# A transformer block on one core: operand sums in steps, keys as side work, elementwise work off GpSimd, recurrence and decays in turn, longer pauses

## The chip, the cores and the metric

The kernel runs on one core of one Trainium2 chip. The metric is device time in microseconds for one execution; the time before is 1280.81 us, the median of three runs (1280.46 to 1280.88). The engines are TensorE (PE, with its weight loads as PEld), VectorE (DVE), ScalarE (ACT), GpSimd (POOL) and SyncE (SP, which here only issues DMAs).

## What is computed

One block on 512 tokens of width 1024, in float32:

```python
x = layer_norm(ALPHA * x + 0.5 * swiglu(x, ffn1_w1, ffn1_w3, ffn1_w2), ln1_g, ln1_b)
x = layer_norm(ALPHA * x + token_mixer(x, w_in, b_in, ...), ln2_g, ln2_b)
x = layer_norm(ALPHA * x + 0.5 * swiglu(x, ffn2_w1, ffn2_w3, ffn2_w2), ln3_g, ln3_b)

# token_mixer
q_a, k_a, v_a, f_h, q_h, i_h, og_h, gate_a, gate_h = split(x @ w_in + b_in)
y_attn = sliding_window_attention(rope(q_a), rope(k_a), v_a, sinks)   # 16 heads of 64, 4 key heads, window 128
o_h = hgrn2_recurrence(silu(q_h), f_h, i_h, lb)                       # 8 heads of 128, chunks of 64
y_h = rms_norm(o_h) * norm_g * silu(og_h)
mix = (sigmoid(gate_a) * (y_attn @ w_pa) + sigmoid(gate_h) * (y_h @ w_ph)) @ w_out
```

The two feed-forward layers have 2816 hidden columns.

## The kernel before, in words

Activations are held with features on partitions and 512 tokens in the free dimension. Every float32 operand of a large product is split into a rounded high part and a remainder (`split`: a copy on ACT into `whi`, then a subtraction on DVE into `wlo`), and a product is three matmuls: high by high, high by low, low by high (`mm3`, or the inner loop of `Quads.mul`).

The wide projections use a seven-product scheme of the Winograd kind on 2x2 blocks (`Quads.quad`): for each pair of 256-column weight groups it loads four raw weight tiles, forms sums of them on DVE (`plus`, tile `wsum`), splits seven operands, and multiplies them in turn with seven forms of the input: the blocks b11, b21, b22 and the sums t1, t2, t3, t4 of blocks. The order of products is f1 (b11), f5 (t1), f6 (t2), f2 (b21), f7 (t3), and, together with the next call's first product, m4 (t4) and m3 (b22). `X` holds the input blocks and their sums; `X.mixed` forms t1 to t4 once for each of the three inputs (first feed-forward, mixer, second feed-forward), with the low parts of t3 and t4 subtracted on POOL. `eight` is the plain first pass of a feed-forward layer, during which `mixed` runs.

The mixer goes through these stages in the code: values and keys (`v_tile`, `k_half`); bias, rotation and split of the keys (`rope`, one multiplication of which is on POOL); `x1.mixed`; the projections of queries (`q_quad`), gates (`gate_quad`) and recurrence inputs (`quad_to`, `vals`); two output projections (`sums`); the last product with its normalization (`down_and_norm`).

Attention and the recurrence are "side work": Python generators in one queue (`Side`). After half and at the end of each product the planner's `tick` adds `rate` times a share to what is due and takes that many steps of the generator; a step that yields `PAUSE` ends that tick's steps, while what is due is kept. `attention` prepares two query tiles (`q_parts`) and interleaves one chunk of score, softmax and value work (`scores`, `probs`, `weigh`) with the next preparation (`both`). `heads` runs, for each head of the recurrence, `decays` (elementwise preparation on DVE and ACT) and then, one head later, `recur` (score products, transposes, updates, output products, a normalization whose inverse root is a `pow` on POOL, transposes, gate). A scheduler then sets, at build time, the order in which each engine's instructions finally stand, from the code's order and its own idea of durations; every engine runs its instructions in that order.

Lines to follow: L71 to L76 `split`; L125 to L149 `fin` and `mixed`; L284 the matmuls of `mul`; L299 `plus`; L304 `keep` (m1, vs, u3: copies of a product's bank by ACT before the bank is used again); L655 to L661 `rope`; L690 to L697 the keys; L721 the query's low part; L738 and L739 scores; L769 the probabilities' scaling; L992, L994 the recurrence's output products; L997 to L1007 its normalization and the transposes behind.

Of the kernel before, what the change touches and what calls it, by code (L numbers as in the profile page):

```python
# [15 lines left out]
ALU = mybir.AluOpType  # L16
# [26 lines left out]
def body(ctx, tc, a):  # L43
# [73 lines left out]
    class X:  # L117
# [8 lines left out]
        def fin(self, n, c, src, eng=None):  # L126
            t = self.op[n][:, :, :, c]
            nc.scalar.copy(out=t[:, 0], in_=src)
            (eng or nc.vector).tensor_tensor(out=t[:, 1], in0=src, in1=t[:, 0], op=ALU.subtract)  # L129

        def mixed(self, room):
            pool = nc.gpsimd
            full = slice(0, 256)
            b11, b12, b21, b22 = (self.plain[k] for k in ("b11", "b12", "b21", "b22"))

            def tmp():
                return room().rearrange("p (k c) -> p k c", k=4)
# [4 lines left out]
            self.fin("t1", full, t1)  # L142
            t4 = tmp()
            nc.vector.scalar_tensor_tensor(out=t4, in0=t2, scalar=-1.0, in1=b21, op0=ALU.mult, op1=ALU.subtract)
            self.fin("t2", full, t2)
            t3 = tmp()
            nc.vector.tensor_tensor(out=t3, in0=b22, in1=b12, op=ALU.subtract)
            self.fin("t3", full, t3, pool)
            self.fin("t4", full, t4, pool)  # L149
# [108 lines left out]
    class Outs:  # L258
# [3 lines left out]
        def room(self, i):  # L262
            return self.rooms[i]
# [4 lines left out]
    class Quads:  # L268
# [63 lines left out]
        def quad(self, src, outs):  # L332
# [3 lines left out]
            p1 = self.plus(w21, w22)  # L336
            p3 = self.plus(w11, w21)
            v, c, m1, vs, u3, p2, p4 = ([] for _ in range(7))
# [10 lines left out]
            def g2():  # L349
                p2.append(self.plus(w22, p3))  # L350
                return wsplit(p2[0])
# [26 lines left out]
            pipe.push(lambda: wsplit(p3), f7)  # L378
            self.late = (v, c, w22, p4, u3, vs, outs)

        def eight(self, src, finish, stages=()):
# [22 lines left out]
            self.x.mixed(self.sum_room)  # L404
# [221 lines left out]
    def quad_to(src, d1, d2, done=None):  # L626
# [5 lines left out]
        quads.quad(src, Outs((*thalves(d1), d2[:, :, 256:]), finish))  # L632
# [48 lines left out]

    top, bot = slice(0, HD), slice(HD, P)
# [546 lines left out]
```

## Time and profile before

| | before |
|---|---|
| median of the runs | 1280.81 us |
| profiled execution: own time | 1279.68 us |
| profiled execution: span, first to last instruction | 1277.8 us |
| PE busy | 1239.9 us, 97% |
| DVE busy | 934.7 us, 73% |
| ACT busy | 628.3 us, 49% |
| POOL busy | 74.1 us, 6% |
| mean granted TensorE clock | 0.995 of full speed |

The profiled execution's own time is 1.88 us above its span, and the median of the runs 1.13 us above that. Matmuls of this kernel overlap with the weight loads of the next ones, so PE counts as busy whenever one of them is under way, and its idle time is where it waits for an operand, a free bank, or nothing at all at the two ends. A row of the timeline gives start and duration in us, engine, line, operation and tiles, and in square brackets the idle time before it and what ended that.

### The profile page before, as it was taken

The page shows a single profiled execution, that of the slowest core. Times are in us where ns is not written, and L with a number is a line of the kernel's source. Part 1 is how long each engine was busy: PE and PEld are TensorE (multiplying, and loading weights), DVE is VectorE, ACT ScalarE, POOL GpSimd, SP SyncE. Part 2 cuts the span into 40 slices and gives each one's busy share as a digit, 9 for nine tenths or more (in the row PEclk, how much of TensorE's full clock was granted, in tenths as well). Part 3 has the DMA queues.
Part 4 walks back from the last instruction along what each step waited for, and adds up shares of the span by engine and source line. Part 5 has one row for each costly group of instructions (what it writes and reads, how often), then busy time and mean ns, then how long its engine had stood idle before and what let it go on. Part 6 is the DMA issues. An engine that isn't in the chain of part 4 may idle for free.

```text
span 1277.8 us, 21726 instructions
## 1 busy us (share of the span) xinstructions
PE 1239.9 (97%) x9040; PEld 1167.8 (91%) x9040; DVE 934.7 (73%) x1288; ACT 628.3 (49%) x891; POOL 74.1 (6%) x53
## 2 busy tenths in 40 slices
PE   8999999999998999999999999999999999999997
PEld 7999999988898999989999988788899999998886
DVE  7987878723399998998778786564898788784325
ACT  5645455511155677687653746442365445462110
POOL 2000000000031100100100010000110000000001
PEclk9999999999999999999999999999999999999998
DMA  6424233523233335223223243664333323343211
GB/s 242 138 95 132 84 116 116 183 97 99 90 112 100 114 118 157 83 87 123 72 78 105 83 148 124 223 206 132 116 101 114 116 92 108 118 162 132 95 38 66
DMA packets 51139, 150.75 MB, mean 118 GB/s; under 512 B 5728, under 2 KB 12896, under 8 KB 51040
## 3 DMA queue, kind: packets, MB, share of 16 engines
q1 hardware_dynamic: 47008, 135.72, 32.6%
q10 hardware_dynamic: 4032, 13.63, 3.0%
q8 instruction: 71, 1.16, 0.4%
q14 instruction: 28, 0.23, 0.1%
HBM read 134.65 MB, written 14.68 MB: 117 GB/s over the span
## 4 chain that ended last, share of the span: by engine, by line
PE 52%; DVE 11%; issue 2%; ACT 2%; POOL 1%; DVEq 0%; POOLq 0%; ACTq 0%
PE A L284 27%; PE A L106 4%; PE A L107 4%; PE A L108 4%; DVE wlo L75 2%; PE B L107 2%; PE B L106 2%; PE B L108 2%; PE B L113 2%; DVE wsum L299 2%; PE B L961 1%; PE B L790 1%; POOL rs L1003 1%; DVE g L721 1%; DVE r L743 1%
## 5 line engine op out<-in xcount | busy, mean ns | idle before, releaser
L284 PE MATMUL A<-x,whi 128*128 128x256 f32 x3840 | 551.2, 286 | 12.2 <-ACT whi L74 6.3
L284 PEld LDWEIGHTS A<-x,whi 128*128 128x128 f32 x3840 | 500.6, 193 | 15.7 <-ACT whi L74 6.6
L75 DVE TENSOR_TENSOR wlo<-raw,whi 128x1024 fp32r<-128x1024 f32 (+1 forms) x186 | 225.6, 1215 | 191.4 <-ACT whi L74 191.2
L74 ACT CAST whi<-raw 128x1024 fp32r<-128x1024 f32 (+1 forms) x186 | 192.7, 1040 | 313.7 <-PE A L108 115.0
L284 PE MATMUL A<-x,wlo 128*128 128x256 f32 x1920 | 312.4, 285 | 1.6 <-DVE wlo L75 1.6
L284 PEld LDWEIGHTS A<-x,wlo 128*128 128x128 f32 x1920 | 267.3, 193 | 2.0 <-DVE wlo L75 2.0
L74 ACT CAST whi<-wsum 128x1024 fp32r<-128x1024 f32 x128 | 134.5, 1051 | 146.3 <-PE A L284 91.5
L75 DVE TENSOR_TENSOR wlo<-wsum,whi 128x1024 fp32r<-128x1024 f32 x128 | 156.2, 1220 | 11.9 <-ACT whi L74 11.7
L106 PE MATMUL A<-whi,x 128*128 128x256 f32 (+1 forms) x360 | 115.7, 321 | 0.0
L107 PE MATMUL A<-wlo,x 128*128 128x256 f32 (+1 forms) x360 | 115.6, 321 | 0.0
L108 PE MATMUL A<-whi,x 128*128 128x256 f32 (+1 forms) x360 | 114.9, 320 | 0.0
L299 DVE TENSOR_TENSOR wsum<-raw 128x1024 f32<-128x1024 f32 x64 | 87.4, 1372 | 2.7 <-POOL x L129 2.0
L299 DVE TENSOR_TENSOR wsum<-raw,wsum 128x1024 f32<-128x1024 f32 x64 | 78.1, 1220 | 0.8
L106 PEld LDWEIGHTS A<-whi,x 128*128 128x128 f32 x360 | 68.5, 190 | 5.0
L108 PEld LDWEIGHTS A<-whi,x 128*128 128x128 f32 x360 | 68.3, 190 | 4.9
L107 PEld LDWEIGHTS A<-wlo,x 128*128 128x128 f32 x360 | 68.5, 190 | 4.5
L107 PE MATMUL B<-wlo,x 128*128 128x512 f32 (+1 forms) x200 | 69.8, 349 | 0.0
L106 PE MATMUL B<-whi,x 128*128 128x512 f32 (+1 forms) x200 | 69.7, 348 | 0.0
L108 PE MATMUL B<-whi,x 128*128 128x512 f32 (+1 forms) x200 | 69.4, 347 | 0.0
L420 POOL TENSOR_TENSOR rstd<-ve,pw 128x1 f32<-128x1 f32 x12 | 16.2, 1351 | 761.2 <-DVE ve L418 760.0
L106 PE MATMUL A<-x,whi 128*128 128x512 f32 (+1 forms) x160 | 59.5, 372 | 0.0
L108 PE MATMUL A<-x,wlo 128*128 128x512 f32 (+1 forms) x160 | 59.3, 371 | 0.0
(171 smaller groups left out, 1520.2 us busy)
## 6 DMA issues: line engine op xcount, KB each, us to landing
raw<-in_w_dram SPq DMA_DIRECT2D x130, 512.0 KB, 3.6
raw<-in_w_fqg_dram SPq DMA_DIRECT2D x24, 512.0 KB, 3.5
raw<-in_w_q_dram SPq DMA_DIRECT2D x8, 512.0 KB, 3.6
raw<-in_w_ga_dram SPq DMA_DIRECT2D x8, 512.0 KB, 3.9
raw<-in_w_gh_dram SPq DMA_DIRECT2D x8, 512.0 KB, 3.7
raw<-in_w_i_dram SPq DMA_DIRECT2D x8, 512.0 KB, 3.9
raw<-in_w_pa_dram SPq DMA_DIRECT2D x8, 512.0 KB, 4.8
g<-x_spill ACTq DMA_DIRECT2D x8, 512.0 KB, 4.8
```

Of the source, the lines that this page charges most:

```text
L74: nc.scalar.copy(out=hi, in_=src)
L75: nc.vector.tensor_tensor(out=lo, in0=src, in1=hi, op=ALU.subtract)
L106: nc.tensor.matmul(out, lhsT=lh, rhs=rh, start=first, stop=False, **kw)
L107: nc.tensor.matmul(out, lhsT=lh, rhs=rl, start=False, stop=False, **kw)
L108: nc.tensor.matmul(out, lhsT=ll, rhs=rh, start=False, stop=last, **kw)
L113: nc.tensor.transpose(out=tp[:, j * P:(j + 1) * P], in_=b, identity=ident)
L284: nc.tensor.matmul(reg, lhsT=w, rhs=x, start=first, stop=last, skip_group_check=True)
L299: nc.vector.tensor_tensor(out=t, in0=x, in1=y, op=ALU.add)
L420: nc.gpsimd.tensor_tensor(out=rstd, in0=ve, in1=pw, op=ALU.pow)
L721: nc.vector.tensor_tensor(out=q[other, h], in0=t[own], in1=q[own, h], op=ALU.subtract)
L743: nc.vector.tensor_tensor_reduce(out=neg[hf][:, i, :kb * P], in0=sc[hf][:, i * 256:i * 256 + kb * P], in1=amask[:, koff:], scale=-(HD ** - ...
L790: mm = nc.tensor.matmul(o[hf][hf * HD:(hf + 1) * HD, i * 256:(i + 1) * 256], lhsT=v_sb[:, n + i + 1 - kb + kk, g * HD:(g + 1) * HD], rhs=p ...
```

## The change

- `X.mixed` becomes a generator of four steps with three given rooms instead of four rooms from a ring; all low parts are subtracted on DVE, and t3 is written over t1. In the feed-forward layers it runs in one go at the place where it ran before; in the mixer its four steps stand between the pushes of the first `quad` (the queries).
- The keys get only their bias at the entry; rotation and split become a generator `k_parts`, side work at rate 1 beside the first gate projection, ahead of `attention` in the queue. The zeroing of the unused key halves moves with it.
- `rope` multiplies by the sine on DVE, not on POOL. After the change POOL keeps the `pow` of the normalizations, the copies of the recurrence and the memsets.
- `probs` pauses twice before its transposes instead of once; `attention` pauses twice before each chunk; `both` takes a preparation step at every third step of the chunk instead of every fourth.
- `recur` pauses after the squares' sum (a plain yield before) and twice, not once, before its last transposes.
- `heads` deals out `recur` of one head and `decays` of the next step by step; before, all of `decays` came first, and then `recur`. The rates of the first three pairs of heads go from 4 to 5.

```diff
-        def mixed(self, room):
-            pool = nc.gpsimd
+        def mixed(self, rooms):
...
-            t1, t2 = tmp(), tmp()
+            t1, t2, t4 = (t.rearrange("p (k c) -> p k c", k=4) for t in rooms)
             nc.vector.tensor_tensor(out=t1, in0=b11, in1=b12, op=ALU.subtract)
+            self.fin("t1", full, t1)
+            yield
...
-            self.fin("t3", full, t3, pool)
-            self.fin("t4", full, t4, pool)
+            self.fin("t4", full, t4)
+            yield
...
+            if not mix:
+                s1()
+                s3()
             pipe.push(lambda: wsplit(w11), f1)
+            if mix:
+                next(mix)
+                s1()
             self.flush()
-            pipe.push(lambda: wsplit(p1), f5)
+            pipe.push(lambda: wsplit(p1[0]), f5)
+            if mix:
+                next(mix)
+                s3()
             pipe.push(g2, f6)
             pipe.push(g4, f2)
+            if mix:
+                next(mix)
+            pipe.push(lambda: wsplit(p3[0]), f7)
+            if mix:
+                next(mix)
...
-    def rope(src, b, sign, dst):
-        nc.scalar.activation(out=dst, in_=src, func=AF.Identity, bias=b, scale=sign)
+    def rope(dst):
         rot = room(0)
         nc.vector.stream_shuffle(out=rot, in_=dst, mask=swap)
-        nc.gpsimd.tensor_tensor(out=rot, in0=rot, in1=sin_t, op=ALU.mult)
+        nc.vector.tensor_tensor(out=rot, in0=rot, in1=sin_t, op=ALU.mult)
...
-    x1.mixed(quads.sum_room)
+    mix = x1.mixed([big(i, [P, 1024]) for i in (2, 4, 10)])
+    k_hi, k_lo = [], []
+
+    def k_parts():
...
+        for j in range(2):
+            t = k_raw[j]
+            rope(t)
+            yield
...
-        yield PAUSE
+        for _ in range(2):
+            yield PAUSE
         tps = [transposed([neg[j // 2][:, j % 2, kk * P:(kk + 1) * P] for j in range(4)]) for kk in range(kb)]
...
         for i in range(4):
+            for _ in range(2):
+                yield PAUSE
             if i < 3:
-                nxt = yield from both(chunk(i // 2, i % 2, qs), q_parts((i + 1) // 2, (i + 1) % 2), 4)
+                nxt = yield from both(chunk(i // 2, i % 2, qs), q_parts((i + 1) // 2, (i + 1) % 2), 3)
...
-    q_quad(0)
+    q_quad(0, mix)
+    side.add(k_parts())
+    side.rate = 1.0
     gate_quad(0)
     pipe.pump()
     side.add(attention())
...
         nc.vector.tensor_reduce(out=ss, in_=sq.rearrange("p (t e) -> p t e", e=P), axis=AX.X, op=ALU.add)
-        yield
+        yield PAUSE
...
-        yield PAUSE
+        for _ in range(2):
+            yield PAUSE
         oT = transposed([on[:, t * P:(t + 1) * P] for t in range(TT)])
...
         for h in (2 * pr, 2 * pr + 1):
-            d = yield from decays(h)
+            if ahead:
+                h0, d = ahead.pop()
+                d = yield from both(recur(h0, *d), decays(h), 1)
+            else:
+                d = yield from decays(h)
             ahead.append((h, d))
-            if len(ahead) > 1:
-                h0, d = ahead.pop(0)
-                yield from recur(h0, *d)
-                yield
+            yield
```

What this does to the order of the instructions is shown at three places, all on DVE, which PE waits for there.

The mixer's entry before, from t3's sum (L147) to the first key's split (L696); `wlo<-raw` is the first weight tile's low part, the r tiles are the keys.

```order
L147 TENSOR_TENSOR wsum<-g_3475,g_3473 128x1024
L299 TENSOR_TENSOR wsum<-raw 128x1024
L621 TENSOR_TENSOR g_3696<-A,bv_c 128x256
L299 TENSOR_TENSOR wsum<-raw 128x1024
L75 TENSOR_TENSOR wlo<-raw,whi 128x1024
L658 STREAM_SHUFFLE r_3933<-r_3931 128x512
L75 TENSOR_TENSOR wlo<-wsum,whi 128x1024
L660 TENSOR_TENSOR r_3931<-r_3931,rope_c_c 128x512
L299 TENSOR_TENSOR wsum<-raw,wsum 128x1024
L661 TENSOR_TENSOR r_3931<-r_3931,r_3933 128x512
L299 TENSOR_TENSOR wsum<-raw,wsum 128x1024
L696 TENSOR_TENSOR g_3925<-r_3931,g_3923 64x512
```

The same stretch now, from t1's low part (x_3477); x_3478 and x_3480 are the low parts of t2 and t3, L138 and L142 their sums.

```order
L75 TENSOR_TENSOR x_3477<-g_3926,x_3477 128x1024
L297 TENSOR_TENSOR wsum<-raw 128x1024
L138 SCALAR_TENSOR_TENSOR g_3927<-g_3926,g_3474 128x1024
L297 TENSOR_TENSOR wsum<-raw 128x1024
L142 TENSOR_TENSOR g_3926<-g_3474,g_3472 128x1024
L75 TENSOR_TENSOR wlo<-raw,whi 128x1024
L637 TENSOR_TENSOR g_3695<-A,bv_c 128x256
L75 TENSOR_TENSOR x_3478<-g_3927,x_3478 128x1024
L75 TENSOR_TENSOR wlo<-wsum,whi 128x1024
L297 TENSOR_TENSOR wsum<-raw,wsum 128x1024
L75 TENSOR_TENSOR x_3480<-g_3926,x_3480 128x1024
L297 TENSOR_TENSOR wsum<-raw,wsum 128x1024
```

The keys' rotation and split have left this stretch, the operand sums stand among the weight sums, and the sum for the third product (`wsum<-raw,wsum`) comes with no key work ahead of it. The first product's low part stands ahead of t2's low part.

The queries of the second half of attention before: shuffle (L658), cosine product (L660), sum (L661), low parts (L721); the sine product between L658 and L661 is on POOL.

```order
L658 STREAM_SHUFFLE r_5613<-g_5130 128x512
L299 TENSOR_TENSOR wsum<-raw 128x1024
L660 TENSOR_TENSOR g_5130<-g_5130,rope_c_c 128x512
L75 TENSOR_TENSOR wlo<-raw,whi 128x1024
L661 TENSOR_TENSOR g_5130<-g_5130,r_5613 128x512
L658 STREAM_SHUFFLE r_5655<-g_5130 128x512
L75 TENSOR_TENSOR wlo<-raw,whi 128x1024
L721 TENSOR_TENSOR g_5618<-g_5130,g_5618 64x512 x2
```

And now, with the sine product as L674.

```order
L673 STREAM_SHUFFLE r_5611<-g_5047 128x512
L297 TENSOR_TENSOR wsum<-raw 128x1024
L674 TENSOR_TENSOR r_5611<-r_5611,rope_s_c 128x512
L675 TENSOR_TENSOR g_5047<-g_5047,rope_c_c 128x512
L75 TENSOR_TENSOR wlo<-raw,whi 128x1024
L676 TENSOR_TENSOR g_5047<-g_5047,r_5611 128x512
L75 TENSOR_TENSOR wlo<-raw,whi 128x1024
L746 TENSOR_TENSOR g_5616<-g_5047,g_5616 64x512 x2
```

One DVE instruction is added for each rotation; the rest keeps its order.

The second of the eight recurrence heads before, from the scaling by the inverse root (L1005), for which PE's transposes wait; L930 to L945 are decays of the head after the next one, L964 the start of the next one's recurrence.

```order
L1005 TENSOR_TENSOR r_7515<-B,rs 128x512
L930 TENSOR_TENSOR g_7543<-r_7540 128x8x64
L937 TENSOR_TENSOR dd<-r_7542 128x4
L938 TENSOR_TENSOR g_6819<-g_6819,r_7542 128x512
L1011 SCALAR_TENSOR_TENSOR r_7535<-B,norm_g_c,g_6414 128x512
L939 TENSOR_TENSOR g_7543<-g_7543,r_7539 128x8x64
L940 TENSOR_TENSOR g_7543<-g_7543,r_7539 128x8x64
L945 TENSOR_TENSOR r_7582<-g_6819,r_7542 128x4x64
L621 TENSOR_TENSOR g_7461<-A,bv_c 128x256
L964 COPY_PREDICATED g_6407<-amask_c,B 128x512
```

The same place now, from L1035, which is that scaling; L956, L960 and L967 are decays of the head after the next one, L994 and L998 the start of the next one's recurrence.

```order
L1035 TENSOR_TENSOR r_7499<-B,rs 128x512
L956 SCALAR_TENSOR_TENSOR r_7547<-rope_c_c,r_7548 128x512
L297 TENSOR_TENSOR wsum<-raw 128x1024
L960 TENSOR_TENSOR g_7550<-r_7547 128x8x64
L297 TENSOR_TENSOR wsum<-raw 128x1024
L1042 SCALAR_TENSOR_TENSOR r_7533<-B,norm_g_c,g_6412 128x512
L994 COPY_PREDICATED g_6405<-amask_c,B 128x512
L998 TENSOR_TENSOR g_7363<-g_7363,r_7362 128x3x64
L967 TENSOR_TENSOR dd<-r_7549 128x4
L637 TENSOR_TENSOR g_7471<-A,bv_c 128x256
```

Those decays are at an earlier point here: their scan (L956) and the work behind it stand after the scaling, and the next head's recurrence starts among them. On PE the number of large matmuls between a head's last output product and its transposes goes, head by head, from 35, 37, 21, 33, 23, 15, 20, 13 to 27, 44, 36, 41, 36, 20, 24, 18 (256 columns each for the first five heads, 512 for the last three).

## Rows read from the trace of the kernel before

**Rows 1.** The page's busy times: us, share of the span, instructions.

```profile
PE 1239.9 (97%) x9040; PEld 1167.8 (91%) x9040; DVE 934.7 (73%) x1288; ACT 628.3 (49%) x891; POOL 74.1 (6%) x53
```

**Rows 2.** PE's waits by line and releaser: us in total, times, longest.

```profile
PE B L113 <- DVE r L1005: 7.7, 8, 1.5
PE A L284 <- ACT whi L74: 6.3, 2, 5.6
PE A L284 <- ACT m L304: 5.6, 3, 3.7
PE B L738 <- DVE g L721: 3.0, 3, 2.2
PE B L113 <- DVE r L769: 2.6, 4, 1.4
PE A L284 <- DVE wlo L75: 1.6, 2, 0.9
```

**Rows 3.** Timeline of PE: stops in both feed-forward layers and the mixer's entry.

```profile
39.08 1.21 PE L284 MATMUL A<-x,whi 128*128 128x256 f32 x8 [1.24 <-ACT m L304]
...
396.27 1.32 PE L284 MATMUL A<-x,whi 128*128 128x256 f32 x8 [3.66 <-ACT m L304]
...
944.52 0.74 PE L284 MATMUL A<-x,wlo 128*128 128x256 f32 x4 [0.64 <-DVE wlo L75]
```

**Rows 4.** Stretches: length, busy us (count) by engine, granted clock, DMA share, GB/s.

```profile
396.00:400.00 4.00, 3.73 (x21) 3.73 (x22) 3.94 (x5) 3.16 (x4) 1.35 (x1) 0.65 0.00 0
400.00:404.00 4.00, 4.00 (x33) 4.00 (x32) 4.00 (x5) 3.69 (x6) 0.00 (x0) 0.92 0.43 131
532.00:536.00 4.00, 3.94 (x23) 3.75 (x24) 3.91 (x7) 1.24 (x2) 0.00 (x0) 0.72 0.47 165
536.00:540.00 4.00, 4.00 (x31) 4.00 (x31) 3.85 (x14) 2.41 (x8) 1.30 (x1) 0.85 0.02 7
```

**Rows 5.** Stretches of attention, output projection and second feed-forward layer.

```profile
420.00:480.00 60.00, 57.50 (x471) 54.57 (x470) 59.15 (x139) 42.55 (x97) 7.13 (x4) 1.00 0.36 118
820.00:830.00 10.00, 10.00 (x45) 8.26 (x44) 6.54 (x6) 6.85 (x8) 0.00 (x0) 1.00 1.00 382
1000.00:1100.00 100.00, 100.00 (x836) 100.00 (x835) 80.09 (x80) 49.58 (x61) 0.00 (x0) 1.00 0.33 106
```

**Rows 6.** Timeline of the mixer's entry: POOL's low parts and DVE's weight sum.

```profile
378.48 6.82 POOL L129 TENSOR_TENSOR x<-wsum,x 128x1024 fp32r<-128x1024 f32 x2 [10.34 <-ACT x L128]
...
382.97 3.40 DVE L299 TENSOR_TENSOR wsum<-raw 128x1024 f32<-128x1024 f32 x1 [1.97 <-POOL x L129]
```

**Rows 7.** Timeline of the second feed-forward layer: the same two.

```profile
936.49 5.76 POOL L129 TENSOR_TENSOR x<-wsum,x 128x1024 fp32r<-128x1024 f32 x2 [10.28 <-ACT x L128]
...
937.14 6.20 DVE L299 TENSOR_TENSOR wsum<-raw 128x1024 f32<-128x1024 f32 x2
```

**Rows 8.** DVE in attention by line: busy us, mean ns, idle before.

```profile
L75 DVE TENSOR_TENSOR wlo<-wsum,whi 128x1024 fp32r<-128x1024 f32 x24 | 29.2, 1216 | 0.4 <-ACT whi L74 0.3
...
L660 DVE TENSOR_TENSOR g<-g,rope_c_c 128x512 f32<-128x512 f32 x8 | 7.2, 903 | 0.0
L661 DVE TENSOR_TENSOR g<-g,r 128x512 f32<-128x512 f32 x8 | 5.5, 682 | 0.0
```

**Rows 9.** Timeline of attention's second half: the longest score wait.

```profile
530.36 2.36 DVE L721 TENSOR_TENSOR g<-g,g 64x512 fp32r<-64x512 f32 x2
...
532.06 0.33 PE L738 MATMUL B<-g,g 128*128 128x128 f32 x1 [2.16 <-DVE g L721]
```

**Rows 10.** Timeline of a head's normalization, from its last output products.

```profile
674.76 0.38 PE L994 MATMUL B<-r,r 128*128 128x128 f32 x2
...
678.59 1.02 POOL L1003 TENSOR_TENSOR rs<-ss,pw 128x4 f32<-128x4 f32 x1 [11.21 <-DVE ss L1001]
...
679.64 0.69 DVE L1005 TENSOR_TENSOR r<-B,rs 128x512 f32<-128x512 f32 x1 [0.81 <-POOL rs L1003]
...
680.39 0.66 PE L113 MATMUL B<-ident,r 128*128 128x128 f32 x4 [0.82 <-DVE r L1005]
```

More of the change, by code (lines that the diff above doesn't have):

```diff
@@ L330, in done, with quad, s1, s3 @@
             pipe.pump()
-        def quad(self, src, outs):
+        def quad(self, src, outs, mix=None):
             w11, w21, w22, w12 = (raw(src[i]) for i in (0, 2, 3, 1))
-            p1 = self.plus(w21, w22)
-            p3 = self.plus(w11, w21)
-            v, c, m1, vs, u3, p2, p4 = ([] for _ in range(7))
+            v, c, m1, vs, u3, p1, p2, p3, p4 = ([] for _ in range(9))
+            def s1():
+                p1.append(self.plus(w21, w22))
+            def s3():
+                p3.append(self.plus(w11, w21))
             def f1(w):
@@ L349, in g2 @@
             def g2():
-                p2.append(self.plus(w22, p3))
+                p2.append(self.plus(w22, p3[0]))
                 return wsplit(p2[0])
@@ L403, in eight @@
             self.mul(c1[1], w[1], "b22", False, True)
-            self.x.mixed(self.sum_room)
+            for _ in self.x.mixed([self.sum_room() for _ in range(3)]):
+                pass
             c2[1] = bank("A")
@@ L684, in body, with q_quad @@
     top, bot = slice(0, HD), slice(HD, P)
-    k_hi = [big(i, dtype=F32R) for i in (4, 10)]
-    k_lo = [big(i, dtype=F32R) for i in (2, 11)]
-    for t in k_lo:
-        nc.gpsimd.memset(t[top, 1].bitcast(F32), 0.0)
-        nc.gpsimd.memset(t[bot, 0].bitcast(F32), 0.0)
-    for j in range(2):
-        t = room(6 + j)
-        rope(accs[j], bias("k", j), 1.0, t)
-        for h, own in enumerate((top, bot)):
-            for half in (top, bot):
-                nc.scalar.copy(out=k_hi[j][half, h], in_=t[own])
-            nc.vector.tensor_tensor(out=k_lo[j][own, h], in0=t[own], in1=k_hi[j][own, h], op=ALU.subtract)
-    x1.mixed(quads.sum_room)
+    k_raw = [room(6 + j) for j in range(2)]
+    for j in range(2):
+        nc.scalar.activation(out=k_raw[j], in_=accs[j], func=AF.Identity, bias=bias("k", j), scale=1.0)
+    mix = x1.mixed([big(i, [P, 1024]) for i in (2, 4, 10)])
+    k_hi, k_lo = [], []
+    def k_parts():
+        k_hi.extend(big(i, dtype=F32R) for i in (4, 10))
+        k_lo.extend(big(i, dtype=F32R) for i in (2, 11))
+        for t in k_lo:
+            nc.gpsimd.memset(t[top, 1].bitcast(F32), 0.0)
+            nc.gpsimd.memset(t[bot, 0].bitcast(F32), 0.0)
+        for j in range(2):
+            t = k_raw[j]
+            rope(t)
+            yield
+            for h, own in enumerate((top, bot)):
+                for half in (top, bot):
+                    nc.scalar.copy(out=k_hi[j][half, h], in_=t[own])
+                nc.vector.tensor_tensor(out=k_lo[j][own, h], in0=t[own], in1=k_hi[j][own, h], op=ALU.subtract)
+                yield
     q_raw = {}
-    def q_quad(pp):
+    def q_quad(pp, mix=None):
         d = [big(i) for i in range(2)]
@@ L705, in done @@
             q_raw[pp] = d
[L706 removed]
+        quad_to(a["w_q"][pp], d[0], d[1], done, mix)
     def q_parts(pp, ip):
@@ L715, in q_parts @@
             t = q_raw[pp][ip][:, i]
-            rope(t, bias("q", 4 * pp + 2 * ip + i), 1.0 if ip == 0 else -1.0, t)
+            nc.scalar.activation(out=t, in_=t, func=AF.Identity, bias=bias("q", 4 * pp + 2 * ip + i),
+                                 scale=1.0 if ip == 0 else -1.0)
+            rope(t)
             yield
@@ L1040, in body @@
     vals(0)
-    next_heads(0, 4.0)
+    next_heads(0, 5.0)
     quad_to(a["w_fqg"][2], pairs[1].q, pairs[1].g)
@@ L1044, in body @@
     pairs[2] = Pair(0)
-    next_heads(1, 4.0)
+    next_heads(1, 5.0)
     quad_to(a["w_fqg"][3], pairs[2].f, pairs[2].q)
@@ L1051, in body @@
     quad_to(a["w_fqg"][4], pairs[2].g, pairs[3].f)
-    next_heads(2, 4.0)
+    next_heads(2, 5.0)
     quad_to(a["w_fqg"][5], pairs[3].q, pairs[3].g)
```

23 lines of the change are left out of this document (9 added, 14 removed).

## The prediction, made before the changed kernel was run

> **What bounds the kernel now.** I read the page's busy times first, then PE's waits, then PE's timeline around each of them, then the stretches for the clock, and last DVE's and POOL's rows at the waits. PE is busy 1239.9 of 1277.8 us [rows 1]: a stop of PE lengthens the run by itself, and what the other engines do counts only where PE waits for it. The span holds 37.9 us without PE. Of this 6.3 us are waits for `whi` [rows 2] at the very start, which the change leaves alone. What it can reach is in the five other lines: 7.7 us before the recurrence's transposes, 5.6 for copies of a bank (m1), 3.0 before scores, 2.6 before attention's transposes, 1.6 for a `wlo` [rows 2]; 20.5 us together. The remaining 11 us are the end of the run and small gaps. The longest are one of 3.66 us at the mixer's entry [rows 3] and one of 2.16 us before scores [rows 9].
>
> Behind these two long stops PE's granted clock is at 0.65, 0.92 and at 0.72, 0.85 in four stretches of 4 us [rows 4], that is, partly at 1.2 instead of 2.4 GHz; everywhere else around it is 1.00. Lost work: 4 x (0.35 + 0.08) = 1.7 us and 4 x (0.28 + 0.15) = 1.7 us. So at most 20.5 + 3.4 = 23.9 us are to be had, which is 1257 us.
>
> In a steady stretch 836 matmuls take 100 us, 0.12 us each [rows 5]; in the output projections, with 512 columns, 45 take 10 us, 0.22 each. These two paces turn counts of matmuls in the new order into time.
>
> **Operand sums.** The change takes two subtractions of 128x1024 per input from POOL and puts them on DVE: 2 x 1.22 = 2.4 us more for DVE [rows 8]. POOL needs 5.8 to 6.8 us for the two [rows 6, 7], and DVE suffers meanwhile: two weight sums that are worth 2.4 us take 6.2 [rows 7], 3.8 lost; at the entry one takes 3.4 instead of 1.2 after 1.97 us of waiting for POOL's result [rows 6], 4.2 lost. So DVE gets back 3.8 to 4.2 for 2.4 and is 1.3 us or more earlier at the next `wlo`. PE's stops behind these places are 1.24 us in the first feed-forward layer, 0.64 [rows 3] and 0.7 (the third of the three waits for m1: 5.6 - 1.24 - 3.66) in the second. The 1.24 and 0.7 are waits for ACT's copy m1, which stands behind a cast of a weight sum that DVE had late; in the new order m1 stands ahead of that cast in the second layer. I take all 2.6 us as gained; bounds 0 and 2.6.
>
> The Trainium skill speaks against the direction of this: "Perfetto Trace Analysis", section "Optimizing Scalar/DVE Operations", says that work of a saturated DVE may be offloaded, even to GpSimd, and adds that the two share a port, so that it might not help. By the first half the moved work would cost DVE 2.4 us per input and 5.5 us for the queries with nothing back, which is the slower case below; rows 7, with 6.2 us for 2.4 us of work, side with the second half.
>
> **The mixer's entry.** Before, the key rotation and split stand among the first product's operands, and DVE reaches the sum for the third product only behind them; PE stops 0.95 us (1.6 - 0.64) for the first `wlo` and 3.66 us for m1. In the new order t1's low part, the weight sums and the first five weight splits come without key work. The first `wlo` is five DVE operations of at most 1.22 us behind t1's low part, without POOL's 4.2 us; the operand of each later product is ready one product (24 matmuls, 2.9 us) or more ahead. I take both stops as gone, 4.6 us, and the clock behind the second, 1.7; bounds 2 and 6.3. Key rotation and split then run beside the first gate product; nothing but attention's first score waits for them, and that comes 24 matmuls later in PE's order than before.
>
> **Attention.** The eight sine products leave POOL: 8 x 0.68 = 5.5 us more on DVE [rows 8], which is full there, 59.15 of 60 us [rows 5]. Back come the cosine products' excess, 8 x (0.903 - 0.682) = 1.8 us [rows 8], and 1.0 us for each pair of low parts that meets a rotation (2.36 instead of 1.36 us [rows 9]). So DVE has 1 to 4 us more in some 180 us, and this is the term with the worst cover. But each rotation becomes shorter by what POOL took over 0.68, and the 2.16 us [rows 9] are just such a chain: its low parts alone end 1.0 us late. Of the score and transpose waits (3.0 + 2.6) I take 3.6 as gained: attention's 16 groups of transposes still stand right behind the last scaling on DVE, and I charge an eighth of a microsecond for each (an estimate from 2.6 us for 16 such groups before, four of which waited). The second clock stretch goes with the 2.16: 1.5 of 1.7. Bounds for the whole: -6 (all that DVE is given, in front of PE) and 7.3. Two more pauses per block and per chunk delay attention; in the new PE order its end is 37 matmuls nearer to the first recurrence head, with main matmuls still between its last steps (21, 14, 12), so nothing is left over that PE would have to wait through.
>
> **The recurrence.** Between a head's last output product and its transposes stand the square, its sum, the `pow`, the scaling, and other DVE work. One head: output products end at 675.14, transposes start at 680.39, so 5.25 us, against 37 matmuls x 0.12 = 4.4 us, and 0.82 us of waiting [rows 10]. DVE itself loses 0.81 us there to the `pow`. The counts change by -8, +7, +15, +8, +13 (x 0.12) and +5, +4, +5 (x 0.22). Setting each new count against its chain, with the new neighbours on DVE, leaves about 0.7, 0, 0, 0.6, 0.1, 1.3, 0, 0 = 2.7 us. What DVE loses to a `pow` does not vanish where PE no longer waits: behind the second head its queue is dense (a scan, two weight sums, then the next head's first steps), and I expect the 0.8 us again before the next transposes. So 7.7 - 2.7 - 0.8 = 4.2 us gained; bounds -1 and 7.7.
>
> **Sum.** 2.6 + 6.3 + 3.6 + 1.5 + 4.2 = 18.2 us. The profiled execution's own time, 1279.68 us, would become 1261.5; it is 1.13 us below the median of the runs, so the median of 1280.81 becomes about 1263 us.
>
> **Rivals.**
> - Nearly everything goes: DVE, no longer held up by POOL, is ahead of PE all through the mixer. For it speaks that seven of the eight heads' counts grow, by 0.8 to 1.8 us, against a mean wait of 7.7 / 8 = 1.0; against it that DVE goes on losing 0.8 us to a `pow` [rows 10]. 1257 us.
> - The waits move: operand sums and entry gain their 8.9 us, but in attention and recurrence each stop that a pause removes comes back at the next score, update or transpose, since DVE is as late as before. For it speaks DVE's 59.15 of 60 us, against it that rows 2 name no wait for an update or an output product. 1272 us.
> - The pauses don't bite: the scheduler fills with the same matmuls as before where the chain is on DVE, as for the sixth head, and the recurrence gains nothing. 1267 us.
> - Slower: DVE becomes the bound from the entry to the end of attention. It is given 2.4 (operands) + 10 x 0.68 (rotations) = 9.2 us in that stretch; if next to nothing comes back from POOL, PE waits that long for `wlo`, the entry's gain is lost with it, and only the recurrence's 4.2 us stand against it: 1286 us. It decides where less than half of the excess in rows 6 to 9 is owed to POOL. By the rule named above it would be the likely one; here rows 6 and 7 show the excess only while POOL runs.
>
> **Chances.** Forecast (1260 to 1266) 0.45; nearly everything 0.15; pauses don't bite 0.13; waits move 0.2; slower 0.05; the rest within a few microseconds of before. The range that leaves out about 2 in 10: 1257 to 1271. A measurement of this kernel tells 0.2% (2.6 us) from no change: faster 0.92, within 0.03, slower 0.05.
>
> **What would show it.** In the new profile: no stop over 0.3 us at the entry and a clock of 1.00 there; no PE wait behind the operand sums; DVE's weight sums at 1.22 us all through; rotations without stretched neighbours; PE's waits for the scaled rows at about 3 us in eight, and for attention's scaling at about 2. Wrong would be: new waits for `wlo` in attention, a wait of PE for the updates (L1016) or for keys, DVE rows as long as before with POOL idle, or PE idle in the mixer as long as before.

## The result, and the profile after

| | before | after |
|---|---|---|
| time, median | 1280.85 us (1280.46 to 1281.72, 4 runs) | 1266.68 us (1265.33 to 1268.93, 4 runs) |
| ratio to before, 95% interval | | 0.9891 [0.9877, 0.9905] |
| profiled execution, own time and span | 1279.68, 1277.8 | 1268.93, 1267.1 |

The changed kernel is 14.2 us (1.1%) faster; 17.8 were forecast (1263), and 1266.68 lies inside the range 1257 to 1271. (The median of before has one run more here than ahead of the prediction.) The profiled execution is the longest of the four. Its own time is 10.75 us below that of before, so what follows is set against 10.75; the spread between runs is taken up in the last section.

The page's busy times of the kernel after answer to [rows 1]: us, share of the span, instructions.

```profile
PE 1239.7 (98%) x9040; PEld 1168.6 (92%) x9040; DVE 929.1 (73%) x1304; ACT 628.5 (50%) x891; POOL 37.5 (3%) x37
```

PE's work is the same; the span without PE goes from 37.9 to 1267.1 - 1239.7 = 27.4 us, 10.5 us less, nearly all of the 10.75. DVE has 16 instructions more and yet 5.6 us less to do.

PE's waits of the kernel after, by line and releaser (us in total, times, longest), against [rows 2]. L282, L113, L763 and L1035 are L284, L113, L738 and L1005 of before; `whi` at the top is again mostly the start of the run (5.79 and 1.15 us; 5.55 and 0.75 before).

```profile
PE A L282 <- ACT whi L74: 7.2, 3, 5.8
PE B L113 <- DVE r L1035: 3.1, 3, 1.3
PE A L282 <- ACT u L302: 1.7, 2, 1.1
PE B L763 <- DVE g L746: 1.7, 3, 1.2
PE B L113 <- DVE g L441: 1.2, 4, 0.4
PE B L991 <- DVE g L970: 0.8, 1, 0.8
PE B L816 <- ACT r L801: 0.7, 1, 0.7
PE A L108 <- DVE wlo L75: 0.5, 1, 0.5
PE A L282 <- DVE g L312: 0.5, 1, 0.5
PE B L113 <- DVE g L998: 0.4, 1, 0.4
PE A L282 <- DVE wlo L75: 0.2, 1, 0.2
```

The waits for `m` (5.6) and for attention's scaling (2.6) are gone as lines; those for the recurrence's scaling fell from 7.7 in eight to 3.1 in three. New lines stand in their place: copies `u` and `r` of ACT, a sum (L312), the start of a head (L991).

Stretches of the kernel after (length, busy us and count of PE, PEld, DVE, ACT, POOL, then granted clock, DMA share, GB/s): the mixer's entry, and the two places with a clock under 1.00 outside the end of the run, against [rows 4].

```profile
395.00:420.00 25.00, 25.00 (x211) 25.00 (x210) 24.85 (x34) 18.11 (x26) 0.00 (x0) 1.00 0.33 106
...
432.00:436.00 4.00, 2.97 (x15) 2.77 (x16) 3.88 (x15) 3.92 (x7) 0.00 (x0) 0.74 0.23 75
436.00:440.00 4.00, 4.00 (x30) 4.00 (x30) 4.00 (x14) 2.69 (x11) 0.00 (x0) 0.83 0.02 6
776.00:780.00 4.00, 2.97 (x21) 2.97 (x22) 2.63 (x5) 0.63 (x1) 0.65 (x2) 0.83 0.22 70
780.00:784.00 4.00, 4.00 (x17) 3.16 (x18) 3.69 (x6) 2.41 (x4) 0.00 (x0) 0.74 0.64 213
```

The entry is now full of PE at full clock (in the same stretch before, 23.60 of 25 us at 0.93). But there are again two stretches partly at 1.2 instead of 2.4 GHz, each worth 4 x (0.26 + 0.17) = 1.7 us, behind other stops than before. In the timeline of PE (start, us, instruction, then the idle time ahead of it and who ended it) these are the first and the last of four rows; the second and third are typical of what attention still waits for:

```profile
432.92 0.33 PE L763 MATMUL B<-g,g 128*128 128x128 f32 x1 [1.22 <-DVE g L746]
...
448.61 1.22 PE L282 MATMUL A<-x,whi 128*128 128x256 f32 x8 [0.68 <-ACT u L302]
...
560.84 1.81 PE L282 MATMUL A<-x,whi 128*128 128x256 f32 x13 [1.07 <-ACT u L302]
...
777.03 0.66 PE L113 MATMUL B<-ident,r 128*128 128x128 f32 x4 [1.32 <-DVE r L1035]
```

Nine such waits between 430 and 565 us (1.22, 0.68, 0.27, 0.70, 0.28, 0.24, 0.46, 1.07, 0.17) make 5.1 us.

DVE by form in the kernel after, from 395 to 600 us (line, engine, names, shapes, count | busy us, mean ns | idle before), against [rows 7, 8]:

```profile
L75 DVE TENSOR_TENSOR wlo<-wsum,whi 128x1024 fp32r<-128x1024 f32 x29 | 35.2, 1215 | 0.3 <-ACT whi L74 0.3
...
L297 DVE TENSOR_TENSOR wsum<-raw 128x1024 f32<-128x1024 f32 x14 | 16.9, 1219 | 1.3 <-DMA raw<-in_w_fqg_dram 1.2
L794 DVE TENSOR_SCALAR r<-r,rd 128x256 f32<-128x256 f32 x48 | 13.9, 350 | 0.1
L746 DVE TENSOR_TENSOR g<-g,g 64x512 fp32r<-64x512 f32 x16 | 11.0, 686 | 0.5
L674 DVE TENSOR_TENSOR r<-r,rope_s_c 128x512 f32<-128x512 f32 x10 | 6.9, 689 | 0.0
...
L675 DVE TENSOR_TENSOR g<-g,rope_c_c 128x512 f32<-128x512 f32 x8 | 5.5, 688 | 0.0
```

Every form has its bare length again: sums 1.22 us, cosine and low parts 0.69. The ten sine products (L674) cost DVE 6.9 us. It is still full: 24.85 of 25 us above, and 58.55 of 60 from 420 to 480 us.

### The profile page after: what moved, and what is told of

Same layout as the page of the kernel before. It is cut to its first block, busy times and chain, and to the rows that moved or that the text cites. A ratio compares the mean times of both kernels' runs of the same rounds, so it can differ in the third digit from the quotient of the medians.

```text
span 1267.1 us, 21689 instructions
## 1 busy us (share of the span) xinstructions
PE 1239.7 (98%) x9040; PEld 1168.6 (92%) x9040; DVE 929.1 (73%) x1304; ACT 628.5 (50%) x891; POOL 37.5 (3%) x37
## 4 chain that ended last, share of the span: by engine, by line
PE 86%; DVE 8%; issue 1%; POOL 1%; DMA 1%; ACT 1%; SPq 0%; DVEq 0%; POOLq 0%; ACTq 0%
PE A L282 50%; PE A L108 6%; PE A L107 6%; PE A L106 6%; PE B L107 4%; PE B L106 4%; PE B L108 4%; PE B L113 2%; DVE wlo L75 1%; PE B L991 1%; PE B L816 1%; POOL rstd L436 1%; DVE g L441 1%; DVE r L768 1%; PE B L763 1%
## 5 line engine op out<-in xcount | busy, mean ns | idle before, releaser
L282 PE MATMUL A<-x,whi 128*128 128x256 f32 x3840 | 546.1, 285 | 9.4 <-ACT whi L74 7.2
L282 PEld LDWEIGHTS A<-x,whi 128*128 128x128 f32 x3840 | 498.4, 193 | 11.6 <-ACT whi L74 7.7
L282 PE MATMUL A<-x,wlo 128*128 128x256 f32 x1920 | 312.4, 284 | 0.2 <-DVE wlo L75 0.2
L282 PEld LDWEIGHTS A<-x,wlo 128*128 128x128 f32 x1920 | 266.5, 193 | 0.9 <-issue 0.4
L297 DVE TENSOR_TENSOR wsum<-raw 128x1024 f32<-128x1024 f32 x64 | 77.6, 1219 | 1.9 <-DMA raw<-in_w_fqg_dram 1.2
L106 PE MATMUL A<-x,whi 128*128 128x512 f32 (+1 forms) x160 | 60.3, 377 | 0.0
L107 PE MATMUL A<-x,whi 128*128 128x512 f32 (+1 forms) x160 | 59.3, 371 | 0.0
```

Of the source, the lines that this page charges most:

```text
L106: nc.tensor.matmul(out, lhsT=lh, rhs=rh, start=first, stop=False, **kw)
L107: nc.tensor.matmul(out, lhsT=lh, rhs=rl, start=False, stop=False, **kw)
L282: nc.tensor.matmul(reg, lhsT=w, rhs=x, start=first, stop=last, skip_group_check=True)
L297: nc.vector.tensor_tensor(out=t, in0=x, in1=y, op=ALU.add)
```

## The experiments

Theory: three things gained. POOL out of elementwise work (operand sums, sine), since POOL and DVE hold each other up ([rows 7]); the order of the mixer's entry; the recurrence's dealing and pauses. What is left is DVE's lateness: in attention because it is full, in the recurrence because it stands behind POOL's `pow`. The rival for each part is named in its expectation. The first six undo one part of the change, the other six try to take away what is left. Ratios are to the kernel before, run on the same chip; the changed kernel's is 0.9891 [0.9877, 0.9905].

**Operands' low parts back on POOL** (the helper that splits a sum hands the engine on)

```diff
-            self.fin("t3", full, t3)
+            self.fin("t3", full, t3, nc.gpsimd)
...
-            self.fin("t4", full, t4)
+            self.fin("t4", full, t4, nc.gpsimd)
```

> The changed kernel, but the low parts of t3 and t4 (2 x 128x1024 per input) are again subtracted on POOL; everything else as in the changed kernel. Theory (POOL and DVE hold each other up): POOL takes 2.9 to 3.4 us for each instead of 1.2, and DVE's weight sums beside it take about 3 us instead of 1.22. The stops of the operand sums come back at least in part, 1.2 to 2.6 us in the two feed-forward layers; at the mixer's entry the low part of t4 is late for the last product, some 1 to 2 us. About 1269 to 1271 us. Rival (only the order of m1 and the steps counts, POOL does no harm): DVE has 7 us less to do, no stop comes back, 1266 us or a little below.

1273.09 us, ratio 0.9933 [0.992, 0.9947]: slower than the changed kernel by 0.42%, 5.4 us, more than expected. In this kernel, POOL's rows by form, and DVE's sums from 910 to 990 us:

```profile
L129 POOL TENSOR_TENSOR x<-wsum,x 128x1024 fp32r<-128x1024 f32 x4 | 12.5, 3144 | 34.9 <-ACT x L128 34.9
...
L129 POOL TENSOR_TENSOR x<-g,x 128x1024 fp32r<-128x1024 f32 x2 | 7.8, 3892 | 18.5 <-ACT x L128 18.5
```

```profile
L298 DVE TENSOR_TENSOR wsum<-raw 128x1024 f32<-128x1024 f32 x8 | 13.7, 1727 | 0.3 <-DVE wlo L75 0.2
```

One form, eight sums: 1727 ns in the mean instead of 1219. Over the whole run DVE is busy 932.8 us, 3.7 more than in the changed kernel, though six operations of 1.22 us were taken from it: 11 us of DVE are lost to POOL's 20.3. PE's stops in this kernel, in the first feed-forward layer, at the entry and before attention's first scores (1.22 us in the changed kernel):

```profile
40.93 2.08 PE L283 MATMUL A<-x,whi 128*128 128x256 f32 x8 [2.06 <-ACT m L303]
...
408.20 1.22 PE L283 MATMUL A<-x,whi 128*128 128x256 f32 x8 [1.60 <-ACT u L303]
...
438.58 0.33 PE L764 MATMUL B<-g,g 128*128 128x128 f32 x1 [1.94 <-DVE g L747]
```

There are two more of 0.88 and 0.73 us in the second layer, and half clock behind the stops at 40.93 and 438.58. Theory holds, the rival (DVE relieved) falls.

**Sine product back on POOL**

```diff
-        nc.vector.tensor_tensor(out=rot, in0=rot, in1=sin_t, op=ALU.mult)
+        nc.gpsimd.tensor_tensor(out=rot, in0=rot, in1=sin_t, op=ALU.mult)
```

> The changed kernel, but the sine product of the ten rotations is again on POOL. Theory (POOL and DVE hold each other up): the cosine products go from 0.69 back to about 0.9 us and the low parts beside a rotation from 0.69 to about 1.2, the rotation's chain is some 1.5 us longer, and attention's waits grow from about 5.1 to 6 or 7 us: 1268 us. Rival (DVE's load counts): DVE gets back 10 x 0.69 = 6.9 us in a stretch where it is full, attention's waits fall to about 3 us: 1264 us.

1270.94 us, 0.9921 [0.9907, 0.9934]: 0.30%, 3.8 us slower. Two views of this kernel, its forms on POOL and DVE from 395 to 600 us, and two of PE's waits:

```profile
L674 POOL TENSOR_TENSOR r<-r,rope_s_c 128x512 f32<-128x512 f32 x10 | 18.7, 1874 | 141.7 <-DVE r L673 106.0 <-DVE rd L791 25.7 <-issue 10.0
```

```profile
L746 DVE TENSOR_TENSOR g<-g,g 64x512 fp32r<-64x512 f32 x16 | 12.9, 808 | 0.5
L675 DVE TENSOR_TENSOR g<-g,rope_c_c 128x512 f32<-128x512 f32 x8 | 7.8, 981 | 0.1
```

```profile
PE B L763 <- DVE g L746: 3.5, 3, 2.0
...
PE B L113 <- DVE r L794: 1.4, 3, 0.6
```

The sine takes 1874 ns in the mean on POOL (689 on DVE), the cosine 981 instead of 688. Scores wait 3.5 instead of 1.7 us, and the waits for the scaling are back (1.4) although all the new pauses are there; those for `u` are gone. In sum attention's waits are 5.6 us from 430 to 565 us, against 5.1, and one of 0.58 us stands ahead of that at 417 us; the expectation had 6 or 7. More of the loss is clock: here the score wait of 2.03 us at 528 us is followed by 0.59 over 4 us, 1.6 us lost in a stretch that has full clock in the changed kernel. DVE had 6.9 us fewer of its own work, yet it is busy 931.4 us instead of 929.1 and PE waited longer, so the load rival falls.

The Trainium skill, "SBUF — State Buffer", section "Who interferes with whom", says that a DVE instruction with two SBUF inputs contends with a GpSimd instruction that reads SBUF. The stretched forms of these two runs (sum, low part, cosine) are of that kind. The same section counts `tensor_scalar` among the operations that can contend, and the scaling L794 of 128x256 agrees: its mean is 383 ns here against 350, because the two of its 48 that ran beside a sine product took 1.38 and 1.04 us, the others 0.35.

**Attention's pauses as before**

```diff
-        for _ in range(2):
-            yield PAUSE
+        yield PAUSE
         tps = [transposed(...
...
-            for _ in range(2):
-                yield PAUSE
             if i < 3:
-                nxt = yield from both(chunk(...), q_parts(...), 3)
+                nxt = yield from both(chunk(...), q_parts(...), 4)
```

> The changed kernel with attention's pauses and interleaving as before (one pause between the scaling and its transposes instead of two, none ahead of a chunk, the next rotation's steps after every fourth step instead of every third). Theory (the pauses took away the waits for the scaled rows): about 2.6 us of waits of PE's transposes for DVE's scaling are back, the other waits of attention stay near 5 us: 1269 us. Rival (a full DVE is late by the same amount wherever PE next asks): waits come back at the transposes and go elsewhere, the sum stays near 5 us: 1266.7 us.

1267.17 us, 0.9893 [0.9879, 0.9907]: no difference that can be told. Two rows of PE's waits in this kernel:

```profile
PE A L282 <- DVE g L312: 2.0, 2, 1.4
...
PE B L113 <- DVE r L794: 0.4, 2, 0.3
```

The transposes' waits for the scaling are 0.4 us in two, not 2.6; instead PE waits 2.0 us for a sum (L312), where it waited 0.5. The rival is right: with the sine on DVE these pauses are worth nothing measurable. So it isn't the pauses that took away the 2.6 us. The sine's move took away at least the 1.4 that come back in the run before this one; whether it took all of them no run shows.

**The entry in the old order**

```diff
-    q_quad(0, mix)
     side.add(k_parts())
-    side.rate = 1.0
+    side.drain()
+    for _ in x1.mixed([quads.sum_room() for _ in range(3)]):
+        pass
+    q_quad(0)
```

> The changed kernel with the mixer's entry in the order of before: both keys' rotation and split, then all four operand sums in one go, then the first query product with its two sums ahead; POOL does no elementwise work here. Theory (the order made both stops at the entry): about 12 DVE operations of the keys and four of the sums stand ahead of the weight sum for the third product, a stop of 3 to 4 us and one of about 1 us, and a stretch at half clock behind them, 1.7 us: 1271 to 1273 us. Rival (POOL's low parts made them, 4.2 us of DVE lost): with the low parts on DVE at 1.2 us each, hardly 1 us of stops, 1267 to 1268 us.

1270.04 us, 0.9919 [0.9906, 0.9931]: 0.28%, 3.6 us slower, without any work on POOL. In the timeline of this kernel the weight sum for the third product starts behind the first key's rotation and split and the two products of the second key's rotation:

```profile
391.50 1.22 DVE L297 TENSOR_TENSOR wsum<-raw,wsum 128x1024 f32<-128x1024 f32 x1
...
392.75 1.05 ACT L74 CAST whi<-wsum 128x1024 fp32r<-128x1024 f32 x1 [2.59 <-DVE wsum L297]
...
393.85 1.44 PE L282 MATMUL A<-x,whi 128*128 128x256 f32 x5 [3.32 <-ACT whi L74]
```

The 3.66 us stop of [rows 3] is back as 3.32, and the clock is at 0.69, 0.50 and 0.96 from 392 to 404 us. So the order makes such a stop without POOL, though with more on DVE ahead of the sum than before: the low parts of t3 and t4 and the keys' sine products. Later the kernel gets part back: the 1.22 us stop at 433 us is missing, one of 1.37 us at 445 us has come, and attention's waits are 3.6 us in sum, at full clock.

**The recurrence as before, and its pauses alone**

```diff
-        yield PAUSE                          # ahead of the pow
+        yield
...
-        for _ in range(2):
-            yield PAUSE                      # ahead of the transposes
+        yield PAUSE
...
-                d = yield from both(recur(h0, *d), decays(h), 1)
...
+                yield from recur(h0, *d)     # behind decays(h), as before
...
-    next_heads(0, 5.0)                       # and two more
+    next_heads(0, 4.0)
```

> The changed kernel with the recurrence as before: decays of a head, then the recurrence of the one before it in one piece, rate 4, one pause between the scaling and its transposes and none behind the sum of squares. Main matmuls between a head's last output product and its transposes are 35, 37, 21, 33, 23, 15, 20, 13 again (now 27, 44, 36, 41, 36, 20, 24, 18). Theory (dealing and pauses gained): PE's waits in the recurrence go from about 4.9 back to about 8 us: 1270 us. Rival (the chain on DVE sets the transposes, whatever the counts): waits stay near 5 us, 1266.7 us.

1271.01 us, 0.992 [0.9908, 0.9933]: 0.29%, 3.7 us slower. The waits for the scaling are near the 7.7 us of [rows 2] again:

```profile
PE B L113 <- DVE r L1035: 7.5, 8, 1.5
```

The theory holds. The second run of this pair keeps the pauses, and undoes the dealing and the rates alone:

> The changed kernel with its pauses in the recurrence but without the dealing (decays, then the recurrence of the head before, rate 4). The counts are 35, 37, 41, 33, 36, 21, 15, 13. If the pauses carry the gain, heads 3 and 5 (41 and 36 matmuls, 4.3 to 4.9 us) lose their waits and the last two (15 and 13) wait about 1 us each: some 4 us of waits, 1266 us. If the dealing carries it, waits are near those of the recurrence before, 7 to 8 us, 1269 to 1270 us.

1267.97 us, 0.9901 [0.9888, 0.9913]:

```profile
PE B L113 <- DVE r L1035: 5.5, 6, 1.5
```

The pauses alone carry two of three parts of the recurrence's gain (0.19% of 0.29%), the dealing, with the rates, about 1.3 us; the intervals overlap, so the split is a rough one. By head the expectation was half right: the fifth head's wait is gone, but the third keeps 0.91 us with 41 matmuls (1.05 with 21), and the last two wait 0.12 and 0.57, not 1.

**The pause behind the `pow`**

```diff
-        yield PAUSE
+        yield
         nc.vector.tensor_scalar(out=ss, ...)
         nc.gpsimd.tensor_tensor(out=rs, ..., op=ALU.pow)
+        yield PAUSE
         on = room(7)
```

> The changed kernel with the pause of the normalization between POOL's pow and DVE's scaling instead of between the sum of squares and the pow. DVE no longer stands behind the pow at 0.8 to 0.9 us per head; the counts become 27, 44, 48, 41, 43, 24, 18, 24. Theory (DVE's loss at the pow is what is left of the recurrence's waits): the waits for the scaling (3.1 us in three heads) fall to 1 us or less: about 1264.5 us. Rival (DVE's full queue is what is left): the waits stay near 3 us and only move to other heads, 1266.7 us.

1272.82 us, 0.9944 [0.993, 0.9959]: slower by 6.8 us, which neither expected, and it did not test what it was made for. DVE still stands 0.81, 0.90, 1.19, 0.90, 1.19 us at the first five `pow`s: a pause moves instructions only where other work is issued in it, and on DVE none was. What it did was to delay the last heads. The seventh now has 18 matmuls of cover instead of 24, and PE waits 2.53 us for its scaling; behind the eighth the output projection's operands come late:

```profile
794.22 0.66 PE L113 MATMUL B<-ident,r 128*128 128x128 f32 x4 [2.53 <-DVE r L1036]
...
823.21 0.80 PE L106 MATMUL A<-x,whi 128*128 128x512 f32 x1 [2.56 <-ACT whi L74]
```

Both stops are followed by half clock (0.50 and 0.70 from 796 to 804 us, 0.50 and 0.78 from 824 to 832). So there is an end to delaying a chain: where its result is the next stage's operand.

**Half of attention's scaling on ACT**

```diff
-            nc.vector.tensor_scalar(out=p_, in0=p_, scalar1=rd[:, j:j + 1], ...)
+            if j % 2:
+                nc.scalar.activation(out=p_, in_=p_, func=AF.Identity, bias=0.0, scale=rd[:, j:j + 1])
+            else:
+                nc.vector.tensor_scalar(out=p_, in0=p_, scalar1=rd[:, j:j + 1], ...)
```

> The changed kernel with every second scaling of attention's weights on ACT (32 operations of 128x128 or 128x256) instead of DVE, 8.7 us of DVE's work. Theory (a full DVE is what is left in attention): its waits fall from about 5.1 to about 3 us, 1264.5 us. Rival (ACT is as late: of the 5.1 us, 1.7 are for its copies u, 0.7 for its copies r): ACT's casts and copies come later by 0.6 us per pair of scalings, the waits stay at 5 us or grow to 7: 1266.7 to 1269 us.

1266.34 us, 0.9886 [0.9873, 0.9899]: no difference from the changed kernel that can be told. In its profile attention's waits are 3.8 instead of 5.1 us: those for `u` are gone, small ones for ACT (0.66, 0.28) have come. That is 1.3 of the 2.1 us that the theory expected; the time alone can't show it.

**A third pause for two heads**

```diff
-        for _ in range(2):
+        for _ in range(3 if h in (0, 3) else 2):
             yield PAUSE
```

> The changed kernel with a third pause ahead of the transposes of two heads, the first and the fourth, where PE waits 0.74 and 1.06 us for DVE's scaling. Main matmuls there go from 27 and 41 to 38 and 53, and 36 becomes 31 for the fifth; the last three stay. Theory (the waits are a count of matmuls that is too small): 11 and 12 matmuls x 0.12 = 1.3 and 1.4 us more cover, both waits go, 1.8 us: about 1265 us. Rival (DVE is late by the same amount wherever PE next asks): the waits turn up at the start of the next head's recurrence or at the fifth head, 1266.7 us.

1265.6 us, 0.9877 [0.986, 0.9893]: 1.8 us less by the ratio, as expected, though the intervals overlap. In the profile both waits (0.74 and 1.06 us) are gone, and one of 0.54 us has come 4 us behind the second (L113 for L998): nearer to the theory, with part of the rival.

**Attention's first chunk later**

```diff
-            for _ in range(2):
+            for _ in range(2 if i else 4):
                 yield PAUSE
```

> The changed kernel with two more pauses ahead of attention's first chunk alone. There PE waits 1.22 us for the last low part of the first query rotation, and its clock is at 0.74 and 0.83 in the 8 us behind. Theory (both come from this one place): the wait and the lost clock, 1.2 + 1.7 = 2.9 us, go: 1263.8 us. Rival (what is late only moves, since DVE is full there until 480 us): other waits of 1 us or more between 433 and 460 us, with or without a clock drop: 1266 to 1267 us.

1266.24 us, 0.9883 [0.9868, 0.9898]: the rival. The stop at 433 us is gone and the clock there is 1.00, but two others stand behind it:

```profile
441.63 0.74 PE L282 MATMUL A<-x,wlo 128*128 128x256 f32 x4 [1.49 <-DVE wlo L75]
...
451.09 0.74 PE L282 MATMUL A<-x,wlo 128*128 128x256 f32 x4 [1.40 <-DVE wlo L75]
```

1.49 + 1.40 for the 1.22 + 0.68 + 0.27 + 0.70 between 430 and 457 us in the changed kernel; attention's waits are 5.1 us in sum in both. Here DVE is full, and PE meets its lateness wherever it next asks.

**No `pow`**

```diff
         rs = mxp.tile([P, TT], F32, name="rs", bufs=2)
-        nc.gpsimd.tensor_tensor(out=rs, in0=ss, in1=pw.broadcast_to([P, TT]), op=ALU.pow)
+        rs = ss
```

> The changed kernel without the pow in the recurrence's normalization (eight instructions of POOL left out; the rows are scaled by the mean square itself, so the output differs). DVE then waits for nothing between the mean and the scaling, where it loses 0.8 to 1.2 us per head now. Theory (that loss is what is left of the waits for the scaling): the three waits of 0.74, 1.06 and 1.32 us fall to under 0.4 us together, 2.7 us: 1264 us. Rival (DVE's other work ahead of the scaling is what is late): they fall by less than 1 us, 1266 us.

1263.9 us, 0.9862 [0.9847, 0.9877]: 3.7 us less by the ratio. One row of the waits in this kernel; then, in the changed kernel, the place where PE waited 1.06 us:

```profile
PE B L113 <- DVE r L1034: 0.3, 1, 0.3
```

```profile
731.60 1.22 DVE L75 TENSOR_TENSOR wlo<-raw,whi 128x1024 fp32r<-128x1024 f32 x1
...
731.83 1.84 POOL L1033 TENSOR_TENSOR rs<-ss,pw 128x4 f32<-128x4 f32 x1 [5.81 <-DVE ss L1031]
733.71 0.69 DVE L1035 TENSOR_TENSOR r<-B,rs 128x512 f32<-128x512 f32 x1 [0.90 <-POOL rs L1033]
```

3.1 us of waits become 0.3, and the 0.44 and 0.52 us at 674 and 818 us go too: of the 4.9 us that are left in the recurrence 3.7 are owed to the `pow`. The 0.84 at the first head's start stay. Where the `pow` runs into a low part of 128x1024 on DVE it takes 1.84 us (1.85 for the sixth head) instead of 1.0; those are the two heads with the longest waits, 1.06 and 1.32.

**Three together** (the edits of the third pause, the later first chunk and half the scaling on ACT)

> The changed kernel with the third pause for the first and fourth head, the two pauses ahead of attention's first chunk, and every second scaling of attention's weights on ACT, together. If each takes away its own waits (1.8 + 2.9 + 1.4 us): about 1261 us. If the waits move within attention: 1264 to 1265 us.

1264.15 us (1262.47 to 1264.32), 0.9865 [0.985, 0.9879]. All its runs lie below all of the changed kernel's, by 2.5 us in the medians and 3.3 by the ratios, whose intervals just touch. It isn't the 6.1 us of the three singly: the later first chunk still has stops of 1.51 and 1.04 us behind it.

## Why the prediction was right, and where it was not

**What bounds.** Right: PE's stops set the time. In the profiled executions 10.5 of the 10.75 us are idle time of PE that went.

**Operand sums, 2.6 us.** Right. The stretch at the first feed-forward layer's stop, before and after:

```profile
36.00:40.00 4.00, 2.76 (x23) 2.55 (x22) 4.00 (x5) 3.98 (x6) 0.00 (x0) 1.00 0.10 20
```

```profile
36.00:40.00 4.00, 4.00 (x36) 4.00 (x34) 4.00 (x6) 3.98 (x6) 0.00 (x0) 1.00 0.02 7
```

From 910 to 990 us PE is busy 79.89 of 80 us, before 78.12; no wait for `m` is left. That POOL was to blame, and not the order of `m` alone, is shown by the first run, where the stops come back with the order kept.

**Entry, 6.3 us.** Right in full: both stops gone, clock 1.00. The old order brings 3.32 us and the half clock back without POOL; POOL's low parts in the new order bring 1.60. Each is enough to stop PE; the prediction had counted them as one cause.

**Attention, 3.6 + 1.5 us.** Here the prediction failed. It forecast 2.0 us of waits left, an eighth of a microsecond behind each of 16 scalings; measured are 5.1, of 5.6 before, and none of them behind a scaling. The step that failed is "attention's 16 groups of transposes still stand right behind the last scaling on DVE": it took the place of the old waits for the place of the lateness. In a stretch where DVE is full the wait is not where the chain is tight but at the next thing PE asks for, be it scores, `u`, a sum or a `wlo`; the runs with old pauses and with a later first chunk show it moving from one to the other at nearly constant size (4.6 and 5.1 us in sum, against 5.1). That DVE's load is the reason is shown for 1.3 of the 5.1 us, which go when half of the scaling leaves it; for the rest it is argued from the constant sum and from DVE's 58.55 of 60 us. It is the rival "the waits move", right for attention's first half, and it was given 0.2 for attention and recurrence together. The clock's 1.5 us failed with it: the half clock left the 2.16 us stop of [rows 9] and came to the 1.22 us one at 433 us. That it came just there is in part chance: in four of the later runs a stop of that length at that place is followed by full clock (last section).

**Contention against load.** The direction was right, and the slower case (0.05) did not come: the 6.9 us of sine on DVE made the kernel faster by 3.8, against the run with the sine on POOL. The pauses in attention, which the prediction counted with this, did nothing measurable.

**The recurrence, 4.2 us.** Right, and in the right places: 0.7, 0.6, 1.3 forecast for the first, fourth and sixth head, 0.74, 1.06, 1.32 measured, zero for the other five. The fourth was put too low: its chain from the last output product to the scaled rows grew from 5.32 to 5.82 us, with a DVE operation of 0.69 us (L367) new ahead of the sum of squares. The reappearance behind the second head was put at 0.8 and came as 0.44 at 674.72 us. Two small waits, 0.85 at the first head's start and 0.52 at 818 us, were not forecast, so 4.9 us are left and not 3.5. Before there were 8.2, with one of 0.43 at 636 us that the forecast left out, so 3.2 were gained. Undoing this part costs 3.7 us. "The pauses don't bite" falls.

**The sum.** For the profiled execution 18.2 us were forecast and 10.75 came. Missing are 3.0 in attention's waits, 1.5 in its clock, 1.0 in the recurrence, 0.6 for longer waits at the very start, and 1.7 for a second half-clock stretch behind the 1.32 us stop at 777 us, which was not forecast; 7.8 against 7.45. The median shows 3.4 us more gain than the profiled execution (14.2 against 10.75); how much half clock the other three executions had, no trace shows. So the time came out inside the range although attention's waits gave 0.6 us and its clock nothing: operand sums, entry and recurrence carry it.

## What to carry to other kernels

Taking elementwise work off a full DVE by giving it to POOL can cost DVE more than the work: compare the same form's mean duration with POOL busy and idle before deciding. Where an engine is full, a wait's place is no guide to its cause, so price the stretch by that engine's load and expect a removed wait at the next consumer; in the recurrence, where the late link was the `pow`, a few more matmuls ahead of the consumer removed most of the wait (1.8 us went with the third pause, 0.54 came back). A pause helps only where other work stands ready to fill it, and not ahead of a result that the next stage reads.

## What the runs showed of the hardware

- The granted clock fell to half level behind stops of 1.2 to 1.3 us, not only behind the 2.16 and 3.66 us of [rows 4], and it did not do so each time. Each kernel of this document has one profiled execution. In nine of them there is a stop of 1.21 to 1.31 us at about 433 us; in five, the changed kernel's among them, half clock follows (0.74 and 0.83 there), in four the clock stays at 1.00. The stop of 1.32 or 1.33 us at about 777 us is there in nine as well, and half clock follows in four. Nor does the length alone decide: between 20 and 900 us, the clock is 1.00 behind each of the thirteen stops of 1.36 to 1.60 us, and it falls behind each of the eight of 1.94 us or more. What decides stays open.
- The four runs of the changed kernel, with the same program, lie between 1265.33 and 1268.93 us. The longest has the lowest mean clock (0.996, the others 0.998), which fits stretches that come in one execution and not in another; the one of 1267.89 us has the clock of the two short ones, so it isn't the clock alone.
- POOL's `pow` of 128x4 takes 1.01 us alone and 1.84 beside a DVE subtraction of two inputs; a subtraction of 128x1024 takes 1.22 us on DVE, 3.1 to 3.9 in the mean on POOL beside DVE's work, and 2.40 at the least. One of 2.40 us began at the entry before at 382.89 us, and DVE's sum of [rows 6], begun 0.08 us behind it, took 3.40: the 2.32 us that POOL still had, and 1.08 more.
